# Gate and query products listed from the fifth column tile on, and three more large buffers, in a two-layer hybrid encoder

## The chip, the cores and the metric

The kernel runs on one core of a Trainium2 chip. The metric is the time of one execution in microseconds of the device. Differences between two kernels are told from runs of both on the same chip.

## What is computed

Two layers of a bidirectional encoder on 1024 tokens of width 1024, in float32. The reference, cut to its order:

```python
for l in range(DEPTH):                       # 2
    h = rms_norm(x, pre_mix_norm[l])
    p = h @ w_in[l]                          # 1024 x 2680 columns
    pa, pb, pc, pd = split_last(p, [A_COLS, B_COLS, C_COLS, D_COLS])
    o = concat([mla_mixer(pa), gqa_mixer(pb), mamba2_mixer(pc), deltanet_mixer(pd)])
    x = x + rms_norm(o @ w_out[l], post_mix_norm[l])
    h = rms_norm(x, pre_ffn_norm[l])
    x = x + rms_norm(conv_ffn(h, f_w_in[l], f_conv_w[l], f_conv_b[l], f_w_out[l]), post_ffn_norm[l])
```

The four mixers are a latent attention (A), a grouped-query attention (B), a state-space scan (C) and a gated delta rule (D). C and D begin with a convolution over tokens of their columns of `p`, and both end with a gate: their result is multiplied with silu of gate columns z. B normalizes and rotates its queries and keys. D needs the inverse of a triangular 64 x 64 matrix for each chunk of 64 tokens, head and direction.

## The kernel before

The transposed normalized activations `hT` lie in SBUF in two parts (a high and a low one, for three products in place of one), in 16 buffers of the large kind. Every dense product takes its operands in such pairs.

Each layer has three stages. The mixer stage runs nine streams of work, `weave` (L1376) merges them: a stream has a start, an end and an offset in `when` (L439), its steps are spread evenly between start and end, and at each turn the stream with the smallest time emits its next step. The number of that turn has no meaning on the chip. What it gives is the order in which the program's instructions are listed. A scheduler then goes through them when the program is built and fixes the order of each engine's queue: of what it holds to be ready at a moment, by its own durations, it takes the instruction with the lowest rank, and the rank is the place in the list. An offset moves a stream's ranks: −719 places its instructions 719 behind where they stand. On the chip each queue runs in the fixed order, and waits where the chip is slower than the scheduler held.

The streams that matter here:

- `T` (`run_T`, L266): ten column tiles of 128 columns for D (q, k, v: tiles 0 to 5) and C (6 to 9). A tile is 48 products into a PSUM tile `p2` of 1024 columns, read out by a convolution (one instruction of ScalarE, two of VectorE, L382), followed by silu, transposes and stores.
- `nats` (L549): the gate columns of C and D and the columns of B, in four chunks of 256 columns. A chunk loads its weights in four parts (`nat_load`, L496: a DMA into `raw`, a copy by ScalarE, a subtraction by GpSimd, into `wn`, one large buffer each), and then makes eight steps of 24 products (`nat_step`, L518, L523), each into a `p2` tile. Gate chunks (the first two) are read out by ScalarE (L562) and VectorE (L563), the chunks of B by ScalarE (L557); every step ends with a store to DRAM.
- `d_prep` (eight steps, L843) makes the matrices of D, `d_inverse` (25 steps, L881) inverts them on VectorE in 15 small steps (L908, L909) and six large products (L917, L918), and ends with 512 small products on PE (L959).
- `prep_a` (eight steps, L1274) makes A's queries, keys and values and stores them; `attend_a` and `attend_b` (`att`, 70 steps) load them (`kn`, L1366) and run the attention; `mixer_c`, `mixer_d` and `prep_b` are the rest.

Buffers: `slots` (L55) gives the number of tiles of 4096, 2048 and 1024 bytes per partition (`s4`, `s2`, `s1`). A tile takes a buffer that is free; if none is, its first instruction waits for the last use of a buffer given up. In the mixer stage `hT` holds 16 of the 34 large ones until the last step of `nats`; others are `wn`, the work tiles of `d_inverse` (`ds`, `nd`, `nn`, `itmp`, `ri`, `ni`), the values `VA` and weights of `prep_a`, and the tiles of attention. PSUM holds two each of `p2` (two banks), `pt` and `p1`.

The asserts in the streams ask that `T` is listed before `mixer_c`, the gates before its second half, and all of `nats` before `prep_b`; both versions keep to them.

Of the kernel before, what the change touches and what calls it, by code (L numbers as in the profile page):

```python
# [32 lines left out]
class Trunk:  # L33
# [18 lines left out]
    def t(self, pool, shape, dt, tag, **kw):  # L52
        return pool.tile(shape, dt, tag=tag, name=self.nm(tag), **kw)

    slots = 34, 12, 24  # L55

    def setup(self):
        nc = self.nc
# [377 lines left out]

class Mix(Trunk):
    deep = dict(y=2, th=2, sT=1, nat=2, K=1, qn=1, p=2, WO=3)
    when = dict(T=(0, 11, 0), nats=(8.58, 18.19, -719), d_prep=(6.5, 7.0, 0),  # L439
                d_inverse=(11.23, 17.34, 0), mixer_c=(16.33, 24.6, 0), prep_a=(13.24, 18.6, 0),  # L440
                att=(19.5, 47.52, 0), mixer_d=(23.21, 43.4, 0), prep_b=(22.4, 32.29, 141))
    par_at = 3
# [1104 lines left out]
```

## Time and profile before

| | us |
|---|---|
| median of 3 runs (lowest, highest) | 3133.91 (3132.33, 3135.88) |
| the profiled execution, its own time | 3137.25 |
| its span in the trace | 3135.5 |
| PE busy | 2987.6 |
| VectorE busy | 1812.3 |
| ScalarE busy | 1233.1 |
| GpSimd busy | 706.4 |
| mean granted clock of PE | 0.973 |

PE is TensorE's products, PEld its weight loads, DVE VectorE, ACT ScalarE, POOL GpSimd, SP the engine that issues DMAs. The profiled execution is one; durations are taken from it, and its time stands beside the span because the span leaves out what lies before the first and behind the last instruction. A busy time is that of the trace: products overlap in PE's pipeline, and their ends are modelled. The granted clock is a share of full speed; it has two levels, 1 and 0.5, and a value between them is the mean of a stretch.

### The profile page before, as it was taken

What the parts mean: (1) busy time and instruction counts of PE and PEld (TensorE: products, weight loads), DVE (VectorE), ACT (ScalarE), POOL (GpSimd) and SP (SyncE); (2) the same over time, 40 slices, a digit from 0 to 9 for tenths busy, and PEclk for the clock granted to TensorE, in tenths of its full rate; (3) what the DMA queues carried; (4) which work ended last, traced back from release to release, by engine and by line L of the source; (5) the groups of instructions that cost most, each with busy time, mean ns of one, the idle gap of its engine ahead of it and who ended that gap; (6) DMA issues with size and microseconds to landing.
All of it is one profiled execution on the core that took longest, in us unless ns stands there. A gap on an engine that the chain in (4) does not pass through costs nothing. (4 is left out here: it accounts for less than half of the span.)

```text
span 3135.5 us, 48510 instructions
## 1 busy us (share of the span) xinstructions
PE 2987.6 (95%) x18206; PEld 2442.3 (78%) x18206; DVE 1812.3 (58%) x3368; ACT 1233.1 (39%) x2607; POOL 706.4 (23%) x1175
## 2 busy tenths in 40 slices
PE   6999998999999999999999999999999999999998
PEld 6778876777888888888787777677778888888886
DVE  3555486585535555555565555866846355555556
ACT  3334355785432222222243434467744322222221
POOL 1255366321200000000043652763211000000003
PEclk9999898999999999999999998999999999999999
DMA  4256533242311111111242554333423121111212
GB/s 136 70 144 162 132 97 89 69 124 80 124 54 41 56 57 50 41 41 56 72 133 71 152 156 128 91 87 77 131 81 108 51 61 54 41 41 48 61 34 114
DMA packets 387053, 267.78 MB, mean 85 GB/s; under 512 B 148320, under 2 KB 355716, under 8 KB 386820
## 3 DMA queue, kind: packets, MB, share of 16 engines
q1 hardware_dynamic: 386820, 264.69, 29.2%
q8 instruction: 144, 2.36, 0.3%
q14 instruction: 89, 0.73, 0.1%
HBM read 195.58 MB, written 68.94 MB: 84 GB/s over the span
## 5 line engine op out<-in xcount | busy, mean ns | idle before, releaser
L263 PE MATMUL p<-hT,wh 128*128 128x512 f32 x3456 | 960.0, 392 | 7.8 <-ACT cy L388 2.6
L263 PEld LDWEIGHTS p<-hT,wh 128*128 128x128 f32 x3456 | 649.1, 189 | 145.3 <-ACT cy L388 3.4
L263 PE MATMUL p<-hT,wl 128*128 128x512 f32 x1728 | 552.9, 391 | 0.0
L263 PEld LDWEIGHTS p<-hT,wl 128*128 128x128 f32 x1728 | 325.3, 188 | 68.4 <-DVE wl L135 0.9
L221 POOL TENSOR_TENSOR acc<-acc,gain 128x768 f32<-128x768 f32 x14 | 28.9, 2065 | 1413.7 <-ACT junk L177 1413.7
L388 ACT ACTIVATE cy<-p,cw 128x1024 f32<-128x1024 f32 x88 | 106.0, 1204 | 594.6 <-PE p L263 594.6
L389 DVE SCALAR_TENSOR_TENSOR cy<-p,cw,cy 128x1023 f32<-128x1023 f32 x88 | 112.8, 1282 | 362.6 <-ACT cy L388 362.4
L523 PE MATMUL p<-wn,hT 128*128 128x256 f32 (+1 forms) x1920 | 293.6, 308 | 28.1 <-DVE pb L563 10.9
L523 PEld LDWEIGHTS p<-wn,hT 128*128 128x128 f32 x1920 | 269.4, 200 | 39.1 <-DVE hT L135 12.5
L133 ACT ACTIVATE wh<-raw 128x512 fp32r<-128x512 f32 x216 | 127.9, 623 | 183.0 <-PE p L263 94.1
L1112 DVE TENSOR_REDUCE nm<-p 128x1 f32<-128x1024 f32 x128 | 155.7, 1219 | 45.4 <-PE p L1110 44.8
L493 PE MATMUL pt<-ident,p 128*128 128x128 f32 x1024 | 153.7, 282 | 12.7 <-DVE qh L135 5.0
L1118 ACT ACTIVATE p<-p,nm 128x1024 f32<-128x1024 f32 x128 | 142.6, 1114 | 54.4 <-DVE nm L1112 35.3
L362 DVE TENSOR_TENSOR acc<-acc,p 128x512 f32<-128x512 f32 x160 | 109.3, 685 | 94.1 <-PE p L358 94.1
L1442 PE MATMUL p<-wo,oh 128*128 128x512 f32 x512 | 162.3, 395 | 0.8 <-ACT oh L133 0.8
L362 DVE TENSOR_TENSOR acc<-acc,pt 128x512 f32<-128x512 f32 x160 | 109.5, 684 | 90.9 <-PE pt L358 88.9
L493 PEld LDWEIGHTS pt<-ident,p 128*128 128x128 f32 x1024 | 118.7, 144 | 44.8 <-issue 7.3
L135 DVE TENSOR_TENSOR wl<-raw,wh 128x512 fp32r<-128x512 f32 x180 | 116.6, 686 | 61.4 <-ACT wh L133 61.4
L358 PE MATMUL p<-owh,gh 128*128 128x512 f32 x352 | 138.4, 393 | 2.7 <-DVE acc L362 2.7
L358 PE MATMUL pt<-owh,gh 128*128 128x512 f32 x352 | 138.0, 392 | 2.9 <-DVE acc L362 2.8
L358 PE MATMUL pt<-owl,gh 128*128 128x512 f32 x352 | 138.0, 392 | 0.0
L358 PE MATMUL p<-owl,gh 128*128 128x512 f32 x352 | 137.9, 392 | 0.0
(321 smaller groups left out, 5322.1 us busy)
## 6 DMA issues: line engine op xcount, KB each, us to landing
raw<-in_f_w_in_dram SPq DMA_DIRECT2D x176, 256.0 KB, 3.2
raw<-in_f_w_out_dram SPq DMA_DIRECT2D x88, 256.0 KB, 2.8
raw<-in_w_in_dram SPq DMA_DIRECT2D x72, 256.0 KB, 3.2
raw<-in_w_out_dram SPq DMA_DIRECT2D x32, 256.0 KB, 3.2
xr<-x_mid SPq DMA_DIRECT2D x16, 512.0 KB, 5.8
x_mid<-xr SPq DMA_DIRECT2D x14, 512.0 KB, 2.7
orow<-o_d SPq DMA_DIRECT2D x48, 128.0 KB, 2.6
pa<-pa_d SPq DMA_DIRECT2D x32, 176.0 KB, 2.8
```

The lines of the kernel that those rows point to most:

```text
L133: nc.scalar.activation(out=hi, in_=src, func=AF.Copy)
L135: (eng or nc.vector).tensor_tensor(lo, src, hi.bitcast(F32), op=ALU.subtract)
L263: nc.tensor.matmul(pm[:, h * 512:(h + 1) * 512], s[:, k % 4, :], self.h_mov(p, k, h), start=a, stop=b)
L358: nc.tensor.matmul(po, s[i // 2][:, tk], w[:, cs], start=a, stop=b)
L362: nc.vector.tensor_tensor(acc[i][:, cs], acc[i][:, cs], po, op=ALU.add)
L388: nc.scalar.activation(out=y, in_=p, func=AF.Identity, scale=w1, bias=b)
L389: nc.vector.scalar_tensor_tensor(y[:, 1:], p[:, :n - 1], w0, y[:, 1:], op0=ALU.mult, op1=ALU.add)
L493: self.nc.tensor.transpose(pt[:n, t, :], src(4 * c + t), self.ident)
L523: self.nc.tensor.matmul(po, self.h_sta(a, k, i), wt[k][b], start=(k == 0 and a == 0 and b == 0), stop=(k == 7 and a == 1))
L1112: v.reduce_max(nm, s, axis=AX.X, negate=True)
L1118: nc.scalar.activation(out=p, in_=s, func=AF.Exp, bias=nm, accum_out=rs)
L1442: nc.tensor.matmul(y[:, cs], s[k // 2][:, k % 2, :], W[k][w][:, cs], start=(k == 0 and s is oh and w == 0), stop=(k == 7 and s is ol))
```

## The change

The stream `nats` is listed from 5.0 to 16.5 instead of 8.58 to 18.19, with the same offset. Its first weights are then listed behind column tile 5 instead of behind tile 8, and its 32 steps over 11.5 units of the list instead of 9.61. The number of large buffers goes from 34 to 37. The room for them, 3 x 4096 bytes per partition, comes from the space for descriptors of DMAs, which is set to 1024 bytes per partition; it was not set before.

```diff
-    slots = 34, 12, 24
+    slots = 37, 12, 24
...
-    when = dict(T=(0, 11, 0), nats=(8.58, 18.19, -719), d_prep=(6.5, 7.0, 0),
+    when = dict(T=(0, 11, 0), nats=(5.0, 16.5, -719), d_prep=(6.5, 7.0, 0),
                 d_inverse=(11.23, 17.34, 0), mixer_c=(16.33, 24.6, 0), prep_a=(13.24, 18.6, 0),
                 att=(19.5, 47.52, 0), mixer_d=(23.21, 43.4, 0), prep_b=(22.4, 32.29, 141))
...
-    nc = _bacc.Bacc("TRN2", target_bir_lowering=False, num_devices=1)
+    nc = _bacc.Bacc("TRN2", target_bir_lowering=False, num_devices=1, dynamic_dma_scratch_size=1024)
```

No instruction is added or taken away in the source.

## Rows read from the trace of the kernel before

**Rows 1.** The page, part 1: busy us, share of the span, instructions.

```profile
PE 2987.6 (95%) x18206; PEld 2442.3 (78%) x18206; DVE 1812.3 (58%) x3368; ACT 1233.1 (39%) x2607; POOL 706.4 (23%) x1175
```

**Rows 2.** Stretches, layer 0: length, busy us by engine (instructions), clock, DMA share, GB/s.

```profile
130.00:204.00 74.00, 64.04 (x373) 51.40 (x372) 43.15 (x108) 30.15 (x46) 36.66 (x39) 0.91 0.37 108
...
254.00:278.00 24.00, 17.82 (x125) 17.41 (x126) 7.77 (x40) 13.08 (x35) 1.48 (x4) 0.86 0.72 148
278.00:365.00 87.00, 87.00 (x605) 75.97 (x604) 57.60 (x97) 29.87 (x72) 44.78 (x118) 1.00 0.51 141
365.00:393.00 28.00, 22.98 (x342) 18.11 (x342) 11.54 (x35) 10.67 (x23) 9.17 (x12) 0.70 0.57 145
...
470.00:496.00 26.00, 19.56 (x113) 12.50 (x111) 16.30 (x35) 7.86 (x21) 19.00 (x35) 0.74 0.21 53
...
860.00:1540.00 680.00, 678.69 (x2994) 561.40 (x2993) 357.69 (x502) 182.61 (x315) 0.00 (x0) 1.00 0.17 50
```

**Rows 3.** The same view, three stretches of layer 1.

```profile
1683.00:1757.00 74.00, 61.95 (x364) 49.74 (x363) 42.64 (x105) 30.36 (x46) 34.51 (x36) 0.91 0.36 105
...
1807.00:1832.00 25.00, 19.25 (x122) 18.58 (x122) 6.96 (x36) 11.71 (x31) 3.07 (x7) 0.80 0.70 145
...
1921.00:1949.00 28.00, 23.20 (x345) 18.18 (x343) 11.25 (x35) 10.69 (x23) 9.32 (x12) 0.70 0.56 144
```

**Rows 4.** Timeline of PE, 130-204: start, us, instruction xcount, idle before it <-releaser.

```profile
137.99 1.09 PE L493 MATMUL pt<-ident,th 128*128 128x128 f32 x8 [1.74 <-POOL th L629]
...
144.04 2.07 PE L263 MATMUL p<-hT,wh 128*128 128x512 f32 x4 [0.87 <-DVE dy L390]
```

**Rows 5.** Timeline of PE from 262 to 396 us.

```profile
268.44 7.29 PE L523 MATMUL p<-wn,hT 128*128 128x256 f32 x40 [4.75 <-DVE pb L563]
275.57 0.27 PE L1313 MATMUL pt<-ident,pa 128*128 128x128 f32 x1
...
301.44 0.96 PE L1325 MATMUL pt<-wukv,lh 128*128 128x512 f32 x3
...
302.84 3.12 PE L523 MATMUL p<-wn,hT 128*128 128x256 f32 x24
...
320.09 0.27 PE L1313 MATMUL pt<-ident,pa 128*128 128x128 f32 x1
...
329.81 11.43 PE L523 MATMUL p<-wn,hT 128*128 128x256 f32 x94
...
368.17 4.62 PE L523 MATMUL p<-wn,hT 128*128 128x256 f32 x24 [2.50 <-ACT pb L557]
...
384.00 1.94 PE L493 MATMUL pt<-ident,kn 128*96 128x128 f32 x8 [1.30 <-DMA kn<-ka_d]
```

**Rows 6.** Waits, 312 to 395 us: who <- for whom: us, times, longest.

```profile
DVE ri L918 <- PE p L523: 14.4, 1, 14.4
```

**Rows 7.** Waits, 1868 to 1952 us.

```profile
DVE ri L918 <- PE p L523: 15.7, 1, 15.7
```

**Rows 8.** Timeline of ScalarE, 321 to 340 us.

```profile
330.00 0.47 ACT L1329 ACTIVATE qa<-pt,rs 128x256 f32<-128x256 f32 x1 [3.38 <-PE pt L1325]
...
338.40 0.84 ACT L1330 ACTIVATE VA<-pt,rs 128x256 f32<-128x256 f32 x2 [0.71 <-PE p L523]
```

**Rows 9.** Timeline of SP's DMA issues, 372 to 386 us.

```profile
379.35 0.43 SPq L1366 DMA_DIRECT2D kn<-ka_d  x1
```

**Rows 10.** The page, part 3: DMA queue, kind: packets, MB, share of 16 engines.

```profile
DMA packets 387053, 267.78 MB, mean 85 GB/s; under 512 B 148320, under 2 KB 355716, under 8 KB 386820
...
q1 hardware_dynamic: 386820, 264.69, 29.2%
```

**Rows 11.** Timeline of ScalarE, 190 to 204 us.

```profile
197.61 1.20 ACT L388 ACTIVATE y<-p,cwv 128x1024 f32<-128x1024 f32 x1
```

**Rows 12.** Timeline of ScalarE, 260 to 270 us.

```profile
264.53 1.94 ACT L898 ACTIVATE nn<-ni 64x1024 f32<-64x1024 f32 x1 [1.48 <-DMA ni<-ni_d]
...
267.55 0.66 ACT L562 ACTIVATE pb<-p 128x256 f32<-128x256 f32 x2
```

**Rows 13.** Timeline of GpSimd, 246 to 250 us.

```profile
247.31 1.29 POOL L135 TENSOR_TENSOR wn<-raw,wn 128x512 fp32r<-128x512 f32 x1 [1.75 <-ACT wn L133]
```

## Prediction

> **What bounds the kernel now.** I read the busy line of the page first, then the tables of busy time by stretch, then single waits. TensorE (PE) is busy for 2987.6 of 3135.5 us, so no more than 148 us can be won by closing idle time, and what the clock loses [rows 1]. Next comes where those microseconds lie. The feed-forward stretch of layer 0 has 678.69 of 680 us busy at full clock, and nothing is to be won there, by more buffers or otherwise [rows 2]. The holes stand in the mixer stage, which runs once in each layer; layer 1 repeats them some 1555 us later [rows 2, 3]. I name four:
>
> - the column tiles, 130 to 204 us: 10.0 us idle in layer 0, 12.1 in layer 1;
> - the front of the gate and query products (I call them N, after `nats`), 254 to 278: 6.2 and 5.8 idle;
> - the handover from N to attention, 365 to 393: 5.0 and 4.8 idle;
> - the end of `mixer_c`, 470 to 496: 6.4 idle in layer 0.
>
> Between the second and the third PE has no hole at all: 87.00 of 87 us [rows 2]. There, order is free to change, and only a shorter sum of work would save time; this change removes no work.
>
> The granted clock adds to the holes. In the handover it is 0.70, so (1 − 0.70) × 2 × 28 = 16.8 us ran at the lower level, 1.2 GHz [rows 2]. What that costs I take from like work at both levels. An N step of 24 products took 3.12 us at the full clock and 4.62 when most of it ran at the low one; eight transposes took 1.09 and 1.94 [rows 4, 5]. So of a low microsecond 0.32 to 0.44 is lost; I use 0.36, nearer to N, which is most of the work. The handover then costs 5.0 + 16.8 × 0.36 = 11.0 us in layer 0 and 10.8 in layer 1, the front of N 6.2 + 6.7 × 0.36 = 8.6 and 5.8 + 10.0 × 0.36 = 9.4, the column tiles 10.0 + 13.3 × 0.36 = 14.8 and 16.8, the end of `mixer_c` 6.4 + 13.5 × 0.36 = 11.3.
>
> The Trainium skill ("TensorE: Matmul & The Clock Gate", Terms) puts the penalty of throttled time at that time times (1 − K/N), here a half. By that rule the handover would cost 5.0 + 8.4 = 13.4 us instead of 11.0, and the saving forecast below would be about 4 us larger. The two pairs of rows say less than a half, because small products are not bound by the clock alone, and the measurement decides.
>
> **Three more large buffers.** A product step of `d_inverse` writes `ri` at line 918. It reads nothing of N, yet VectorE stood idle 14.4 us before it and 15.7 us in layer 1, until an N product ended [rows 6, 7]. That is not a data dependency. The tile needs an s4 buffer, and one came free only when N's third weight chunk had been used. `prep_a` shows the same: ScalarE reads the keys of a block out at 330.00 us, but the values beside them, into a new `VA` tile, only at 338.40, behind an N product [rows 8]. The code makes two `ri` tiles and one `VA` there: three tiles waited, and three buffers are added. Meanwhile PE ran 94 N products in a row from 329.81 to 341.24 with nothing of the other streams between them [rows 5].
>
> That stall costs PE nothing while it lasts. What it costs comes at the handover. The inverse and the last steps of `prep_a` end late, and the first key tile `kn` of attention is loaded only at 379.35 [rows 9], though N's last step begins at 368.17 [rows 5]. PE then waits for `kn` and starts its transposes at 384.00, in low clock [rows 5]. If `ri` and `VA` come up to 14 us sooner, the inverse's small products fall among N's last steps, the inverse's own tiles come free before N ends, and `kn` can be in place by then. I bound this term by 0 (the buffers go elsewhere) and by the whole handover, 11.0 + 10.8 = 21.8 us, and take two thirds, 14.5: some of the wait for `kn` and the first exponentials has no cover either way.
>
> Giving up the descriptor space costs nothing that I can see: 264.69 of the 267.78 MB that DMA moved went through one queue of kind hardware_dynamic [rows 10].
>
> **The products earlier in the list.** The offset of −719 sets N's rank 719 instructions behind its place in the list. Counting from the source (48 products for a column tile, 39 instructions for a `d_prep` step of which eight follow, 27 for an N step), N's first instruction ranked behind `d_inverse`'s ninth step and `prep_a`'s first; now it ranks just behind column tile 8 and ahead of tile 9. Its last step moves from behind attention's sixth step to about its third.
>
> In the column tiles' own holes this moves little. Both large PSUM buffers (`p2`, two of them) are taken there: tiles 3 and 4 wait to be read out, and tile 5 starts at 144.04 only when VectorE has read one [rows 4]. Later ScalarE reads tile 6 out only at 197.61, where tile 7 holds the other buffer [rows 11]. An N step needs such a buffer too, and the tiles up to 8 rank above it. So I take 0 of the 14.8 + 16.8 us. Its bounds are 0 and half of it, 16, if N should get in ahead of a tile.
>
> In the front of N the rank should help. PE waits 4.75 us before 268.44 for N's read-out on VectorE [rows 5]; that one waits for ScalarE, which ran `d_inverse`'s copies first (from 264.53, the first of 1.94 us) and N's read-out at 267.55 [rows 12]. With N ahead of `d_inverse` in rank, the read-outs should stand before these copies. But ScalarE also stood waiting for the DMA of `ni` in that place, 1.48 us, and the order is fixed when the program is built, by durations that need not be those of the chip. Bounds 0 and 8.6 + 9.4 = 18.0; I take half, 9.
>
> What else moves: each of N's 16 weight loads puts a DMA on SP's queue, a copy on ScalarE, and a subtraction of 1.29 us on GpSimd [rows 13]. If six of them move to before 204 us, that is 6 × 1.29 = 7.7 us more on GpSimd, which is busy for 36.66 of those 74 us [rows 2]. Behind them would queue the masks of `d_prep` and the scaled queries that PE waits for in the tile stage; the cover is the stall of 14 us that `d_inverse` no longer has. Uncovered, it is up to 7.7 us in a layer; I take 1.5 in all. N's read-outs and stores are the same in number, and go past `prep_a`'s rather than behind.
>
> **The sum.** −14.5 − 9 + 1.5 = −22 us. Against the profiled execution, 3137.25 us (its span is 3135.5), this gives 3115.2; that execution stands 3.3 us over the median of the runs, so the time is 3133.9 − 22 = 3112 us. With the bounds, this case runs from about 3094 (both terms whole) to 3127 (just outside what can be told from no change).
>
> **Rivals.** (1) Nothing is won: PE is saturated from 278 to 365 us, and N, which ends sooner, merely gives its place to `prep_a`. For it speaks that hole-free stretch, against it the three tiles that wait in both layers. 3134, within 6. (2) Slower. N now ranks above `prep_a` and `d_inverse`, and runs ahead of both; it ends sooner, and their last steps stand alone, with nothing to fill PE. Place: the handover. Price: `prep_a`'s first transposes stand at 275.57 and, five steps on, at 320.09, a round of 8.9 us [rows 5]. Its twelve PE instructions, at no more than 0.32 us (three of the widest took 0.96), are 3.8 us of it [rows 5]. A step left alone leaves 5.1 us idle, and its 3.8 at the low level lose 0.36 ÷ 0.64 of that, 2.1, more. Two to three such steps cost 14.4 to 21.6 us in a layer; less the 4.5 that the front still wins, 10 to 17. I take 12, which is 24 in all: 3158. It decides if N's last step ends more than one round ahead of `prep_a`'s last. For it speaks that PE did run 94 N products on end when it could; against it, that N's last four steps still rank among attention's first. (3) The column tiles' holes are filled too, because N takes a PSUM buffer ahead of a tile: 16 us more, 3096. Against it stands the late read-out of tile 6.
>
> **How the numbers follow.** Forecast 0.45, rival 1 0.20, rival 2 0.23, rival 3 0.12. A difference under 0.2% (6 us) can't be told from no change here. Faster: 0.45 + 0.12 = 0.57; same 0.20; slower 0.23. The range goes from 3086 (rival 3 with part of what the two terms leave) to 3146, half way into rival 2, and leaves out about 0.15. The forecast's own range is 3094 to 3127.
>
> **What would show it.** Right: no wait of `ri` or `VA` for an N product; `kn` issued before N's last step ends; less than 3 us idle in the handover, at a clock above 0.85; the front of N without the 4.75 us hole; the holes of 130 to 204 us unchanged. Wrong: N ends well ahead of the inverse and PE stands cold behind it; or new waits for GpSimd in `d_prep`. The forecast fails as a whole if the new order shifts the attention and `mixer_d` stretch, which I count as rigid; no row of before says how a new order would fall out there.

## The result, and the profile after

The changed kernel takes 3164.12 us (median of five runs, 3155.25 to 3166.46); the kernel before, run beside it, 3133.57 (3132.33 to 3135.88). The ratio is 1.0089 with a 95% interval of 1.0074 to 1.0103: slower by 28 us by the ratio (the medians differ by 30.6), where 22 us faster were forecast, and outside the range. The profiled execution took 3160.45 us, its span is 3158.7, so 23.2 us more than the span before.

The first look is again at the busy line of the page (after):

```profile
PE 2997.7 (95%) x18206; PEld 2444.1 (77%) x18206; DVE 1811.4 (57%) x3368; ACT 1232.7 (39%) x2607; POOL 709.4 (22%) x1175
```

The instructions are the same in number as in [rows 1], and no engine but PE does 4 us more. PE's busy time rose by 10.1 us with the same products; as the stretches below show, more of them ran at the low clock. The rest is idle time.

To place it, I cut the mixer stage of each layer into four stretches that begin at the same work, counted from the first product of the first column tile: −4 to 170 us (column tiles), 170 to 290 (N and the rest of the inverse), 290 to 345 (handover) and 345 to 700 (attention). The columns are those of [rows 2]. Before, layer 0 and layer 1:

```profile
70.00:244.00 174.00, 162.94 (x984) 134.62 (x983) 95.87 (x230) 62.70 (x98) 78.48 (x85) 0.96 0.38 109
244.00:364.00 120.00, 112.68 (x809) 100.39 (x808) 66.13 (x140) 47.60 (x124) 52.45 (x130) 0.97 0.57 149
364.00:419.00 55.00, 48.59 (x494) 37.48 (x494) 31.26 (x76) 26.17 (x53) 21.15 (x29) 0.84 0.40 105
419.00:774.00 355.00, 330.87 (x3037) 251.37 (x3036) 244.86 (x556) 225.05 (x534) 148.06 (x263) 0.96 0.34 95
...
1623.00:1797.00 174.00, 160.85 (x972) 132.98 (x971) 95.92 (x227) 62.31 (x96) 77.99 (x85) 0.96 0.38 107
1797.00:1917.00 120.00, 113.54 (x791) 100.36 (x789) 65.98 (x143) 47.76 (x123) 52.59 (x126) 0.96 0.54 146
1917.00:1972.00 55.00, 48.80 (x508) 37.87 (x508) 28.74 (x73) 24.74 (x51) 22.71 (x35) 0.84 0.43 114
1972.00:2327.00 355.00, 335.08 (x3070) 254.74 (x3069) 248.04 (x563) 228.17 (x541) 146.81 (x263) 0.97 0.34 96
```

The same stretches after:

```profile
69.00:243.00 174.00, 157.35 (x979) 132.19 (x978) 86.60 (x214) 60.59 (x103) 73.31 (x80) 0.95 0.38 109
243.00:363.00 120.00, 112.61 (x783) 99.45 (x782) 80.29 (x163) 47.55 (x110) 58.93 (x124) 0.97 0.54 140
363.00:418.00 55.00, 49.01 (x505) 35.14 (x504) 26.28 (x65) 25.14 (x56) 24.39 (x41) 0.91 0.44 120
418.00:773.00 355.00, 331.07 (x3013) 250.50 (x3013) 239.40 (x552) 224.46 (x529) 145.11 (x259) 0.95 0.34 92
...
1630.00:1804.00 174.00, 156.11 (x961) 130.84 (x960) 88.06 (x221) 60.11 (x101) 76.43 (x83) 0.94 0.38 108
1804.00:1924.00 120.00, 112.76 (x763) 98.73 (x762) 72.00 (x138) 45.59 (x106) 51.73 (x113) 0.96 0.54 139
1924.00:1979.00 55.00, 48.51 (x465) 35.16 (x463) 22.14 (x67) 20.57 (x48) 20.84 (x40) 0.72 0.38 110
1979.00:2334.00 355.00, 333.85 (x3063) 251.94 (x3062) 247.27 (x565) 230.96 (x542) 149.41 (x268) 0.96 0.33 93
```

Each row gives a cost as in the prediction: length less PE's busy time, and 0.36 of the time at the low clock, (1 − clock) × 2 × length. The first row after has 174 − 157.35 = 16.7 us idle and 17.4 us low, so 22.9; before it was 11.1 + 0.36 × 13.9 = 16.1. Summed over both layers:

| cost, us | tiles | 170 to 290 | handover | attention | sum |
|---|---|---|---|---|---|
| before | 34.2 | 19.8 | 25.3 | 61.9 | 141.3 |
| after | 48.3 | 20.7 | 27.1 | 68.1 | 164.2 |
| after less before | +14.1 | +0.9 | +1.8 | +6.2 | +22.9 |

The sum grew by 22.9, the span by 23.2. So the loss is placed: most of it stands in the column tiles, where the forecast expected nothing, and the handover, where it expected 14.5 us, gave none. Each cell comes from one execution. How far it can be trusted shows in e3_scratch below, which has the order of instructions of before on every engine: its cells are 35.7, 18.4, 24.3 and 62.0, within 1.5 us of before. The +6.2 of attention is less sure, because the clock is printed in hundredths; summed over windows of 5 us it is +4.7.

In the tiles, PE's timeline of layer 0 (after) shows what is new:

```profile
157.72 0.39 PE L523 MATMUL p<-wn,hT 128*128 128x256 f32 x1 [1.19 <-ACT wn L133]
159.06 4.87 PE L523 MATMUL p<-wn,hT 128*128 128x256 f32 x25 [0.96 <-POOL wn L135]
...
176.48 2.08 PE L263 MATMUL p<-hT,wh 128*128 128x512 f32 x4 [7.46 <-DVE pb L563]
```

N's first two steps run at 157.72, ahead of column tile 6, and tile 6 (176.48; before at 157.5) then waits 7.46 us, 5.03 in layer 1, until VectorE has read out an N step. ScalarE's timeline of the same place says why so late:

```profile
170.31 0.62 ACT L133 ACTIVATE wn<-raw 128x512 fp32r<-128x512 f32 x1
171.12 0.63 ACT L133 ACTIVATE wh<-raw 128x512 fp32r<-128x512 f32 x1 [0.19 <-DMA raw<-in_w_in_dram]
171.92 0.63 ACT L133 ACTIVATE wh<-raw 128x512 fp32r<-128x512 f32 x1 [0.18 <-DMA raw<-in_w_in_dram]
172.46 0.64 ACT L562 ACTIVATE pb<-p 128x256 f32<-128x256 f32 x2
```

N's products were done by 168.6, but its read-out (L562) stands behind the copies of weights (L133), which wait for transfers; and on SP's queue (its DMA issues) the tiles' own weights, L247, came after N's, L509:

```profile
165.23 1.76 SPq L509 DMA_DIRECT2D raw<-in_w_in_dram  x2
167.08 5.81 SPq L247 DMA_DIRECT2D raw<-in_w_in_dram  x4
```

In layer 1 that is the whole wait: VectorE takes its part (L563) as soon as ScalarE is done. In layer 0 some 3 us come on top. ScalarE has read the first step by 172.8, VectorE comes to it only at 176.02, because small instructions stand ahead of it that take seven times as long while GpSimd subtracts weights (rows of VectorE and of GpSimd):

```profile
172.55 1.19 DVE L158 TENSOR_SCALAR rs<-rs 128x8 int32<-128x8 int32 x1
...
176.02 0.41 DVE L563 SCALAR_TENSOR_TENSOR pb<-pb,p 128x256 f32<-128x256 f32 x1
...
172.45 2.48 POOL L135 TENSOR_TENSOR wl<-raw,wh 128x512 fp32r<-128x512 f32 x2
...
179.01 0.17 DVE L158 TENSOR_SCALAR rs<-rs 128x8 int32<-128x8 int32 x1
```

In this whole trace VectorE's 128 x 8 instructions take 0.17 us in the median where GpSimd runs nothing beside them (246), and 1.13 us where they overlap a subtraction of L135 (30).

The last column tile ends at 284 us instead of 234, and `prep_a` begins at 296.70 instead of 275.57 [rows 5]. At the front of N the wait of [rows 5] is still there, and a second one behind the last tile (PE, layer 0, after):

```profile
268.73 4.55 PE L523 MATMUL p<-wn,hT 128*128 128x256 f32 x24 [4.08 <-DVE pb L563]
...
288.22 5.15 PE L523 MATMUL p<-wn,hT 128*128 128x256 f32 x41 [1.16 <-DVE y L390]
...
296.70 0.27 PE L1313 MATMUL pt<-ident,pa 128*128 128x128 f32 x1
```

The waits for a buffer of [rows 6] and [rows 8] are gone. VectorE (after) writes `ri` without the stall, though no sooner than before (336.24), as the work ahead of it comes later:

```profile
337.08 2.33 DVE L918 TENSOR_REDUCE ri<-itmp 128x128 f32<-128x1024 f32 x2
```

and ScalarE writes `VA` right behind the keys, not 8 us later [rows 8]:

```profile
343.31 0.48 ACT L1329 ACTIVATE qa<-pt,rs 128x256 f32<-128x256 f32 x1 [0.27 <-PE pt L1325]
343.68 0.47 ACT L1330 ACTIVATE VA<-pt,rs 128x256 f32<-128x256 f32 x1
```

But `prep_a` now ends last. In layer 1, N's last step ends at 1935.8, `prep_a`'s last transposes begin at 1945.36, and PE waits 4.00 us for the key tile, with the clock low from 1941 to 1972, 0.50 (PE, layer 1, after):

```profile
1945.36 0.47 PE L1313 MATMUL pt<-ident,pa 128*128 128x128 f32 x1
...
1962.73 1.92 PE L493 MATMUL pt<-ident,kn 128*96 128x128 f32 x8 [4.00 <-DMA kn<-ka_d]
```

### The profile page after: what moved, and what is told of

Its sections match the earlier page's. It is cut to its first block, busy times and chain, and to the rows that moved or that the text cites. A ratio compares the mean times of both kernels' runs of the same rounds, so it can differ in the third digit from the quotient of the medians.

```text
span 3158.7 us, 48471 instructions
## 1 busy us (share of the span) xinstructions
PE 2997.7 (95%) x18206; PEld 2444.1 (77%) x18206; DVE 1811.4 (57%) x3368; ACT 1232.7 (39%) x2607; POOL 709.4 (22%) x1175
## 5 line engine op out<-in xcount | busy, mean ns | idle before, releaser
L263 PE MATMUL p<-hT,wh 128*128 128x512 f32 x3456 | 959.8, 392 | 19.8 <-DVE pb L563 12.5
L523 PE MATMUL p<-wn,hT 128*128 128x256 f32 (+1 forms) x1920 | 297.8, 309 | 32.1 <-DVE hT L135 11.1
L523 PEld LDWEIGHTS p<-wn,hT 128*128 128x128 f32 x1920 | 271.1, 201 | 43.1 <-DVE hT L135 13.4
L133 ACT ACTIVATE wh<-raw 128x512 fp32r<-128x512 f32 x216 | 127.9, 623 | 188.0 <-PE p L263 95.1
L135 DVE TENSOR_TENSOR wl<-raw,wh 128x512 fp32r<-128x512 f32 x180 | 116.8, 686 | 62.4 <-ACT wh L133 62.2
L358 PE MATMUL p<-owh,gl 128*128 128x512 f32 x352 | 138.0, 392 | 0.0
```

The lines of the kernel that those rows point to most:

```text
L133: nc.scalar.activation(out=hi, in_=src, func=AF.Copy)
L135: (eng or nc.vector).tensor_tensor(lo, src, hi.bitcast(F32), op=ALU.subtract)
L263: nc.tensor.matmul(pm[:, h * 512:(h + 1) * 512], s[:, k % 4, :], self.h_mov(p, k, h), start=a, stop=b)
L358: nc.tensor.matmul(po, s[i // 2][:, tk], w[:, cs], start=a, stop=b)
L523: self.nc.tensor.matmul(po, self.h_sta(a, k, i), wt[k][b], start=(k == 0 and a == 0 and b == 0), stop=(k == 7 and a == 1))
```

## The experiments

The change has three parts: buffers, an earlier start in the list, an earlier end. The first four runs take them apart. Each diff is against the whole change.

**e1_slots**, the buffers and the descriptor space alone; **e2_nats**, the list places alone; **e6_start** and **e7_end**, buffers with one end of the stream moved.

```diff
# e1_slots
-nats=(5.0, 16.5, -719)
+nats=(8.58, 18.19, -719)
# e2_nats
-slots = 37, 12, 24
+slots = 34, 12, 24
-num_devices=1, dynamic_dma_scratch_size=1024
+num_devices=1
# e6_start
-nats=(5.0, 16.5, -719)
+nats=(5.0, 18.19, -719)
# e7_end
-nats=(5.0, 16.5, -719)
+nats=(8.58, 16.5, -719)
```

> The three buffers and the descriptor space alone; the products stand in the list where they stood before. Theory A (the loss comes from the place in the list: N's steps get their PSUM buffer in the order of the list, so that they stand between the column tiles, stretch these, and make prep_a late): no loss here, 3112 to 3136 us, the tiles end at about 234 us as before, the waits of ri and VA gone. Rival B (the loss comes from the buffers and the new order they bring, or from the smaller descriptor space): 3155 to 3170 us. Rival C (the loss comes from the earlier end of N, ahead of prep_a's last steps): as A.

> The new place in the list alone (5.0 to 16.5), with 34 large buffers and the descriptor space as before. Theory A: as slow as the whole change or slower, 3158 to 3185 us, with the column tiles ending near 284 us and prep_a's first transposes at 295 us or later. Rival B: 3128 to 3140 us. Rival C: 3158 to 3170 us.

> Whole change, but N ends at 18.19 in the list as before (5.0 to 18.19). Theory A: the tiles are stretched as in the whole change, since still two or three N steps stand between two tiles; 3150 to 3170 us. Rival B: 3155 to 3170 us. Rival C: 3112 to 3138 us, as N's end is back.

> Whole change, but N begins at 8.58 in the list as before (8.58 to 16.5). Theory A: the tiles are whole again (end near 234 us), prep_a starts near 275 us; 3110 to 3140 us. Rival B: 3155 to 3170 us. Rival C: N still ends early and leaves prep_a's last steps alone; 3150 to 3170 us, with the clock low for 25 us or more at the handover in layer 1.

The last four columns are costs of both layers, as above.

| | median us | ratio to before (95%) | tiles | 170 to 290 | handover | attention |
|---|---|---|---|---|---|---|
| e1_slots | 3130.10 | 0.9983 (0.9973 to 0.9993) | 36.1 | 16.8 | 9.0 | 67.5 |
| e2_nats | 3153.24 | 1.0061 (1.0046 to 1.0076) | 48.6 | 12.4 | 26.9 | 68.9 |
| e6_start | 3140.77 | 1.0022 (1.0012 to 1.0032) | 43.3 | 19.2 | 7.1 | 69.7 |
| e7_end | 3144.20 | 1.0035 (1.0022 to 1.0048) | 35.7 | 14.5 | 22.8 | 70.9 |

With N as before the buffers don't cost, they win 4 us, so B doesn't explain the loss. But with N's new places they do cost: e2, without them, is 10.9 us faster than the whole change (0.0028 of the ratio, 9 us), and the difference stands between 170 and 290 us, 12.4 there and 20.7 in the whole change. Why was not found. In e2 the waits of `ri` and `VA` for an N product are gone too, so the new places alone remove them. The start alone adds 10.7 us to e1, the end alone 14.1, both 34.0, which is 9 more than their sum and also not explained. Theory A, which put all on the start, is half right, and so is C: e6 and e7 lie between their ranges, and e2 lies below both. The stretches keep start and end apart: the start adds 7.2 us in the tiles and nothing at the handover; the end adds nothing in the tiles and 13.8 us at the handover. These are the handover rows of e1_slots, layers 0 and 1:

```profile
362.00:417.00 55.00, 52.92 (x441) 40.36 (x440) 36.92 (x82) 27.42 (x57) 27.72 (x38) 0.94 0.39 113
...
1907.00:1962.00 55.00, 51.69 (x503) 40.41 (x502) 35.77 (x86) 27.42 (x60) 22.89 (x31) 0.97 0.40 112
```

and of e7_end:

```profile
364.00:419.00 55.00, 48.37 (x430) 34.88 (x428) 31.41 (x73) 27.76 (x61) 24.37 (x42) 0.97 0.33 97
...
1920.00:1975.00 55.00, 49.88 (x348) 34.06 (x348) 30.14 (x73) 23.38 (x51) 24.01 (x41) 0.75 0.33 96
```

In e1_slots `prep_a`'s last step is over 30 us before N's last product, and the key tile is asked for before N ends. SP in e1_slots, layer 0:

```profile
349.05 0.38 SPq L1338 DMA_DIRECT2D ka_d<-qa  x1
...
361.68 0.43 SPq L1366 DMA_DIRECT2D kn<-ka_d  x1
```

and PE, N's last product:

```profile
369.90 0.38 PE L523 MATMUL p<-wn,hT 128*128 128x256 f32 x1
```

In e7_end `prep_a`'s last transposes come 8.1 and 9.4 us after N's last product, in the whole change 1.2 and 10.0.

**The rank.** Built with an offset of −1600 in place of −719, both the kernel before and the changed one have the same order of instructions on all five engines. At −719 the products are already the last choice among what is ready. Yet PE's order in the changed kernel is tile 5, N 0 and 1, tile 6, N 2 to 4, tile 7, N 5 to 7, tile 8, N 8 to 10, tile 9: the order of the list, in which 0.35 units part two N steps and 1.0 two tiles. Tiles and N steps share the two `p2` buffers, and here they got them in the order of the list: the lowest rank didn't put N behind the tiles.

**e9_p1** takes N's steps out of `p2`; **e10_load** moves only the loads of the first weight chunk to 5.0: fifteen empty turns stand between them and the first step.

```diff
# e9_p1
-        po = self.p2([128, DM])[:, :n]
+        po = (self.p1([128, 512]) if n == 256 else self.p2([128, DM]))[:, :n]
# e10_load
-nats=(5.0, 16.5, -719)
+nats=(5.0, 16.52, -719)
-        yield
+        for _ in range(16):
+            yield
-nats=(self.nats(l, P), 33)
+nats=(self.nats(l, P), 48)
```

> The whole change, but N's steps write into the small PSUM kind p1 and not into p2, which leaves p2 to the column tiles. Theory A1 (the early start costs because N's steps take p2 in the order of the list and so push the column tiles, and what follows them, back): tiles end before 255 us in layer 0 instead of 284, prep_a's first transposes before 287 us instead of 297; the time falls to 3135 to 3155 us; some cost stays, since d_prep uses p1 too and now queues behind N. Theory A2 (it costs through the weight loads: raw buffers, ScalarE's and GpSimd's splits ahead of those of the tiles): tiles still end after 270 us and the time stays at 3155 us or more.

> Whole change, but of the early start only the first weight chunk's loads are listed at 5.0; the steps stand from 8.6 to 16.5. Theory A1: no cost from the loads, tiles end near 234 us, the time is that of the version with the end at 16.5 alone, 3138 to 3150 us. Theory A2: the tiles end 10 us or more later than in that version, and the time is 3152 us or more.

e9_p1: 3187.32 us, 1.0171 (1.0153 to 1.0190). In layer 0 the last tile is read out by 249 us instead of 288 and `prep_a` begins at 253 instead of 297, as A1 said, so the order in `p2` is shown to push them back. But the time got worse, against A1: `d_prep` shares `p1`, its last exponential comes 11 us later, and PE idles 20.0 of the 120 us from 244 on (7.4 after; in both layers that stretch costs 63.2, against 20.7). So e9 shows what the order in `p2` does to the tiles, and not what it costs.

e10_load: 3151.02 us, 1.0057 (1.0037 to 1.0077), 6.8 us over e7_end; the last tile is read out 16 and 14 us later than there, which is A2's sign. The loads alone delay the tiles: their stretch costs 58.3 (35.7 in e7_end; the others 8.8, 23.9 and 66.3). The time lies between what the two theories gave. The start costs 20 us over e7_end. Some 7 of them come with the loads, which the intervals of the two runs hardly tell from nothing (0.0022 of the ratio, each of them ±0.0013 to ±0.0020), the rest with the steps.

**e11_prepa_e7** and **e12_prepa_after** list `prep_a` earlier by as much as N's end, **e13_prepa_e1** does so with N as before; **e8_after8** ends N later.

```diff
# e11, e12, e13
-prep_a=(13.24, 18.6, 0)
+prep_a=(11.55, 16.91, 0)
# e11
-nats=(5.0, 16.5, -719)
+nats=(8.58, 16.5, -719)
# e13
-nats=(5.0, 16.5, -719)
+nats=(8.58, 18.19, -719)
# e8
-nats=(5.0, 16.5, -719)
+nats=(8.58, 20.08, -719)
```

> Buffers, N from 8.58 to 16.5, and prep_a listed as much earlier as N's end (11.55 to 16.91 instead of 13.24 to 18.6). Theory A3 (the early end costs because prep_a's last steps come after the last of N, with nothing of N to fill PE): prep_a's last transposes come before N's last step, the first score product 10 us or more earlier than with the end alone, and the time falls by 10 to 20 us to 3122 to 3136. Rival (N's early end costs whatever prep_a does, since attention's first steps then lack N as filling): no more than 4 us gained, 3140 to 3148 us.

> The whole change, and prep_a listed earlier by as much as N's end (11.55 to 16.91). Theory A3: the handover is mended, N's last steps lie behind prep_a's last, and the time falls by 10 to 20 us, to 3142 to 3155; what is left over the kernel with the buffers alone (12 to 20 us) is the cost of the early start. Rival: no more than 4 us gained, 3158 to 3168 us.

> Buffers, N as before (8.58 to 18.19), prep_a listed earlier (11.55 to 16.91). Theory A3: with N's end as before, prep_a's last steps already lie ahead of N's last, so nothing more is won at the handover: 3124 to 3134 us. Rival (prep_a's lead itself is worth time, whatever N does): 3110 to 3122 us.

> Buffers, N from 8.58 to 20.08, its end as much later as the change put it earlier. Theory A3 (what counts is that N outlasts prep_a; more lead is of no use): 3126 to 3136 us, handover as with the buffers alone. Rival (each step of N that is later fills a hole): 3110 to 3122 us.

| | median us | ratio to before (95%) | tiles | 170 to 290 | handover | attention |
|---|---|---|---|---|---|---|
| e11_prepa_e7 | 3133.77 | 1.0004 (0.9992 to 1.0015) | 37.1 | 14.9 | 15.4 | 68.3 |
| e12_prepa_after | 3153.56 | 1.0062 (1.0047 to 1.0077) | 41.9 | 22.9 | 24.9 | 67.2 |
| e13_prepa_e1 | 3130.79 | 0.9990 (0.9979 to 1.0002) | 36.1 | 17.2 | 7.2 | 73.1 |
| e8_after8 | 3135.66 | 1.0012 (1.0003 to 1.0022) | 46.6 | 22.7 | 3.1 | 69.6 |

A3's times hold: with `prep_a` ahead of N's end again, 10.4 us come back in e11 and 10.6 in e12 (9.7 and 8.5 by the ratios); where N outlasts `prep_a` already (e13), nothing is won. In e11 the gain stands at the handover, 22.8 to 15.4. In e12 only 2.2 us of it stand there, though A3 had the handover mended, so for the whole change A3 rests on the time and not on the place. e8 has the cheapest handover of all, 3.1, and is still 5.6 us over e1: its tiles and the stretch behind them cost more (46.6 and 22.7), with N beginning at the same place of the list. That was not traced.

**e3_scratch**, the kernel before with the descriptor space of 1024 and nothing else:

```diff
-num_devices=1
+num_devices=1, dynamic_dma_scratch_size=1024
```

> The descriptor space alone set to 1024, with the instruction order of every engine as before. Step of the prediction (the space costs nothing): within 0.1% of before, 3131 to 3137 us. Rival (less room for descriptors slows transfers): 3138 us or more.

3133.84 us, 1.0006 (0.9997 to 1.0015): the space costs nothing that these runs can tell.

**e14_raw8**, the whole change with eight `raw` buffers instead of four (in all eight lines that name them), paid with two large ones. They hold weights in flight, and also `prep_b`'s columns, which it reads back from DRAM (L1207):

```diff
-slots = 37, 12, 24
+slots = 35, 12, 24
...
-"raw", bufs=4
+"raw", bufs=8
```

> The whole change with eight raw buffers for weight loads instead of four; the room comes from two of the three new large buffers (35 instead of 37). Theory A2 (of the early start, the loads cost: N's eight raw tiles hold the four raw buffers, and the tiles' own weights come late): the hole of 7.46 us ahead of column tile 6 falls below 3 us in both layers, and PE's idle time from the first column tile to 170 us behind it falls from 16.6 and 17.9 to 14 or less; time 3145 to 3158 us. Theory A1 (PSUM order alone): the hole stays above 5 us, time 3160 us or more.

3129.93 us, 0.9991 (0.9982 to 1.0001): all of the loss is gone, more than either theory said, and not in the expected way. The hole ahead of tile 6 only falls to 4.46 and 2.84 us; the cost of the tiles falls by 7.4, that of attention by 14.6 (68.1 to 53.5). So four runs repeat the study with eight `raw` buffers and 35 large ones (the diff is against e14_raw8), N's places as in e1, e6 and e7, and `prep_a` as in e13.

```diff
# e15, e18
-nats=(5.0, 16.5, -719)
+nats=(8.58, 18.19, -719)
# e16
-nats=(5.0, 16.5, -719)
+nats=(5.0, 18.19, -719)
# e17
-nats=(5.0, 16.5, -719)
+nats=(8.58, 16.5, -719)
# e18
-prep_a=(13.24, 18.6, 0)
+prep_a=(11.55, 16.91, 0)
```

> Eight raw buffers and 35 large ones, N and all else listed as before: the control for the whole change with eight raw buffers, which measured 3130 us. Theory A2 (the raw buffers mattered because of the early start): this version gains nothing from them, 3126 to 3134 us, as the version with three large buffers alone. Rival D (eight raw buffers are worth some 15 us in attention's stretch, whatever N does, and the early and short N still costs its 20 to 34 us): 3098 to 3116 us.

> As the control, but N from 5.0 to 18.19. Theory A2: within 4 us of the control. Rival D: 8 to 16 us slower than the control, as with four raw buffers (10.7 us).

> As the control, but N from 8.58 to 16.5. If the early end costs because prep_a's last steps stand alone (A3), raw buffers don't touch it: 10 to 18 us slower than the control. Otherwise within 4 us of it.

> As the control, with prep_a listed earlier (11.55 to 16.91). By A3 no gain beyond the control's, within 4 us of it, since N outlasts prep_a there already.

| median us | N as before | start early | end early | both |
|---|---|---|---|---|
| four raw, 37 large | 3130.10 | 3140.77 | 3144.20 | 3164.12 |
| eight raw, 35 large | 3102.06 | 3123.16 | 3120.37 | 3129.93 |

The profiled execution of e15, from which its stretches are, took 3113.06 us, 11 over its median. Rival D holds: the `raw` buffers are a gain of their own, and under it N's new places still cost 28 us (34 with four). **e15_raw8_base is faster than both kernels**: 0.9907 (0.9886 to 0.9927) of before, and 62 us under the changed one. The start costs 21 us there and the end 18 (e16 0.9968, e17 0.9958), 21 being more than D said; together they cost less than their sum. e18, 3116.36 us, 0.9948 (0.9934 to 0.9963), is 14 us slower than e15, and nothing in A3 says so: its handover costs 33.4 us against 16.3. Its trace shows the wait for a buffer again, `DVE ri L918 <- PE p L523: 5.4, 1, 5.4`, in both layers, which e15 doesn't have. `prep_a` stores its last keys 19 us ahead of N's end (364.1 in layer 0), yet `kn` is asked for 11 us behind it, after loads of `mixer_c` (L751) that wait for PE. SP in e18, layer 0:

```profile
344.86 0.73 SPq L1338 DMA_DIRECT2D ka_d<-qa  x1
...
373.39 0.32 SPq L751 DMA_DIRECT2D bt<-bn_d  x1
...
375.50 0.43 SPq L1366 DMA_DIRECT2D kn<-ka_d  x1
```

**e19_raw8_34** and **e20_raw10_34** ask whether the large buffers carry any of that gain. Against the kernel before:

```diff
# e19
-"raw", bufs=4
+"raw", bufs=8
# e20
-"raw", bufs=4
+"raw", bufs=10
# both
-num_devices=1
+num_devices=1, dynamic_dma_scratch_size=1024
```

> Eight raw buffers, 34 large ones as before, N listed as before: the raw buffers alone. If the 28 us between the control with eight raw buffers (3102) and the version with three large buffers (3130) is theirs alone: 3098 to 3110 us. If a third large buffer is needed for the handover (the wait of ri for an N product comes back, and costs the handover up to 16 us): 3112 to 3122 us.

> Ten raw buffers, 34 large ones, N listed as before: all of the room that the descriptor space gives, spent on raw buffers. If the weight loads still wait for raw buffers at eight, faster than with eight and 34 by 5 us or more; if eight are enough, within 4 us of it.

e19: 3107.58 us, 0.9920 (0.9903 to 0.9937). e20: 3120.03 us, 0.9952 (0.9936 to 0.9968). Raw buffers alone bring 25 us. The one large buffer brings 5.5 more, which lies within the two intervals, so only the stretch speaks for it: the handover costs 24.2 in e19, much as before (25.3), and 16.3 in e15, and `ri` waits 10.4 us for an N product in e19, not in e15. These are the handover rows of e19_raw8_34:

```profile
365.00:420.00 55.00, 49.60 (x507) 37.54 (x507) 39.18 (x105) 29.78 (x63) 28.77 (x39) 0.88 0.47 131
...
1897.00:1952.00 55.00, 49.62 (x487) 37.41 (x486) 37.37 (x98) 27.22 (x57) 24.77 (x34) 0.78 0.42 114
```

Ten `raw` buffers are 12 us worse than eight, neither of what was expected. The handover costs 34.1, 9.9 more than in e19, the stretch before it 4.0 and attention 3.4 more. In its trace the first weights of the output product (L1414) are asked for at 376.71, right behind `kn`, 73 us sooner than in e19. Whether they are the cause stays open.

**What sorts the handover.** In these runs it is the moment at which `kn` is asked for, counted from the end of N's last product. In seven traces (e1, e6, e8, e11, e13, e15, e16) this is at most 3.9 us behind it in both layers, and the handover costs 3.1 to 16.3. In the other thirteen it is 5.9 to 22.4 us behind, and the handover costs 19.8 to 34.1. In seven of the thirteen (the whole change, e2, e7, e9, e10, e14, e17) `prep_a` stores its last keys 3.7 us or more behind N's end, as A3 says. In the other six (before, e3, e12, e18, e19, e20) it does so ahead of it, and there the inverse's last small product comes 8.3 to 16.1 us behind N's end (at most 6.0 in the seven cheap ones). So A3 is one of two ways to a late `kn`; the other is a late inverse. This is read from the traces, and no run was made to part the two.

Where the `raw` buffers bring their time is shown in stretches only: from before to e19, 7.6 us in the tiles and 18.6 in attention. For the tiles, a row that speaks for it stood in the trace of before all along. SP's waits from 69 to 290 us, before:

```profile
SPq L247 <- POOL wl L135: 43.2, 14, 5.9
...
SPq L509 <- POOL wl L135: 15.7, 4, 12.7
```

and in e15_raw8_base:

```profile
SPq L509 <- POOL wl L135: 33.9, 5, 13.9
SPq L247 <- POOL wl L135: 21.7, 10, 6.0
```

SP stood still for the tiles' weight buffers for 43.2 us in 14 waits, with all other issues queued behind; with eight buffers, 21.7 in 10. But its waits with N's loads rise from 15.7 to 33.9, so the queue stands little less in all; the row points to the weight buffers, and doesn't prove how they save time. For attention, what the traces show is that `prep_b`'s loads move: with four buffers the last of them comes in the midst of attention, with eight ahead of that stretch. SP in before and in e19_raw8_34:

```profile
503.31 0.38 SPq L1208 DMA_DIRECT2D raw<-pb_d  x1
...
374.19 0.52 SPq L1208 DMA_DIRECT2D raw<-pb_d  x1
```

The weights of the output product follow it, at 523.8 and 449.8. Which of these transfers matters was not tried.

## Why the prediction was wrong, step by step

**The handover term, −14.5 us.** As a mechanism it was right: with the buffers alone the waits for `ri` and `VA` are gone, `kn` is asked for before N's last step, and the handover's cost falls from 25.3 to 9.0, so by 16.3. (The rows show one wait of each in a layer; the third tile was counted from the code.) What failed is that it was taken to survive the second edit. The end at 16.5 takes it back (22.8 in e7_end, 27.1 in the whole change). `prep_a` then ends last, and in layer 1 the key tile is asked for 2.8 us behind `prep_a`'s last key store; in layer 0 it is 6.4 us, with eight loads of `mixer_c` between. With N's new places the buffers even cost 9 to 11 us (the whole change against e2), which no term and no rival had. And of those 16.3 us only 4 reach the time of e1: attention costs 5.6 more in its profiled execution, which is also 5 us under the median of its runs, where that of before is 3 over.

**The front of N, −9 us.** It measured +0.9. The step that failed is "the rank should help". N was the last choice among what is ready before and is so after; the lower offset shows it. What moved N is the list place, by the buffers of `p2`. In e2 the stretch did fall, by 7.4, so with 34 large buffers the new places gave about what was forecast, for another reason, and the three buffers took it back; how stays open.

**The column tiles, 0, with bounds of 0 and a gain of 16.** They lost 14.1 us. The step "the tiles up to 8 rank above it" took rank for what hands out `p2`. Rival 3 had N get in ahead of a tile, which happened, but gave it the wrong sign: it does not fill the old holes (PE's four waits from 134 to 144 us are 4.7 us after and 5.4 before; N is listed behind tile 5), it makes a new one and puts 11 N steps of 3.1 us ahead of the last tile, where one stood before. That bound excluded a loss without a reason.

**GpSimd and the loads, +1.5 us.** Under-sized: the first chunk's loads alone cost about 7 us (e10_load, hardly clear of noise). The price was sought in GpSimd's own 1.29 us. What the traces show in its place are the `raw` buffers and the queue that the loads share with the tiles' weights, and VectorE's small instructions, which took 1.13 instead of 0.17 us beside a subtraction and gave some 3 of the 7.46 us ahead of tile 6 in layer 0.

**Rival 2, 3158 us with a chance of 0.23,** was the nearest. Its place was right, `prep_a`'s last step alone at the handover, and its condition, that N ends more than a round of 8.9 us ahead, was met in layer 1 (10.0) and not in layer 0 (1.2). Its reason, N's rank, was wrong, and its price of 24 us was too high for that part: 14.1 us by e7_end less e1. The rest of the loss is the start and what the two edits cost together, which no rival had with that sign. So the nearness of its 3158 is in part luck.

**Attention as a rigid stretch.** It gave +6.2 us (+4.7 in finer windows), and −18.6 in e19 with other buffers. It is not rigid.

**Of the signs named:** no wait for `ri` or `VA`, right. It doesn't speak for the buffers, though, since e2 lost the same waits without them. `kn` before N's end, right in e1 and wrong in the whole change (388.05 us, N's end 374.1). Under 3 us idle in the handover at over 0.85, likewise (2.1 and 3.3 us at 0.94 and 0.97 in e1; 6.0 and 6.5 at 0.91 and 0.72 after). The front without its hole, wrong: 4.08. The tiles' holes, unchanged but for the new one.

**The clock's price of 0.36** held in 18 of 19 executions. Beside that of before, idle time plus 0.36 of the low time in the four stretches gives the change of the span within 4.2 us in all but e9_p1, where it gives 10.6 too much. With the half that the Trainium skill ("TensorE: Matmul & The Clock Gate", Terms) gives, the 18 sums miss by up to 10.8, and that of e9_p1 by 18.5.

## What to carry to other kernels

Where instructions share a rotating buffer, the place in the list decided here who goes first, and the lowest rank didn't undo it: before moving a stream in the list, write down who takes the buffers of its PSUM, of its weights in flight and of its stores in that order. When two edits come together, price the first one with the second in place: three buffers that win 4 us alone cost 9 to 11 with the other edit. Look also for what stands ahead of a transfer on its queue: the key tile was late behind `prep_a`'s store in some runs and behind `mixer_c`'s loads in others. And a load queue that stands for buffers is worth a trial before anything is reordered; here 8 KB of each partition, spent on `raw` buffers, brought 25 us where 12 KB of large buffers brought 4.

## What had not been expected

Four more `raw` buffers of 2 KB per partition, off the critical chain as the views were read, won 0.8%. And small changes move this kernel by 12 to 14 us in a way that their reason didn't foresee (e18 against e15, e20 against e19), so a single variant's gain of that size says little of the mechanism that it was built for.
